# Extra matmuls on zeros in layer 1, with weights at four places behind the moving operand

## The chip, the core and the metric

The kernel runs on one core of one Trainium2 chip. The metric is the device time of one execution in microseconds (us). The engines are TensorE (PE: matmuls, and PEld: its weight loads), VectorE (DVE), ScalarE (ACT), GpSimd (POOL) and SyncE (SP, which issues the large DMA transfers).

## The reference

The kernel computes two layers of a bidirectional encoder on a sequence of 256 positions of width 1024, all in float32. In each layer

```python
h = rms_norm(x, g_mix)
b_a, c_a, x_a, u_p, q, k, v, ga, gp, gt = split(h @ w_in)
y_a = short_conv_mixer(b_a, c_a, x_a, conv_w, w_a_out)
y_p = multiscale_pool_mixer(u_p, w_pool, pool_scale)
y_t = windowed_gqa(q, k, v, rel_bias, sink) @ w_attn_out
x = x + (sigmoid(ga) * y_a + sigmoid(gp) * y_p + sigmoid(gt) * y_t) @ w_o
gate, up = split(rms_norm(x, g_ffn) @ w_gu)
x = x + (silu(gate) * up) @ w_down
```

and after both layers one more RMS norm. The input projection `w_in` is 1024 x 8704, and the feed-forward width is 2816.

## The kernel before, in words

Activations are held transposed: 128 features on the partitions, all 256 positions along the free dimension. A weight tile is a block of 128 x 128. One product of PE takes such a block as its stationary operand (the weights) and a tile of 128 x 256 as its moving operand, and adds 128 x 256 to an accumulator in PSUM.

To keep float32 accuracy with the faster float32r format, each operand is split in two: `hi`, the value rounded to float32r (by ACT, line 139), and `lo`, the remainder (by DVE, line 140). `mm3` (lines 164 to 168) makes three products of each block: hi weights by hi data (line 166), hi by lo (167) and lo by hi (168). The weights come from DRAM in the order of use, 16 blocks to a transfer (`dma_chunk`, issued by SP), and are split 8 blocks at a time (`convert`). Three buffers hold raw chunks, five each hold `hi` and `lo` parts. The order of the weights is a plan written out by `plan_layer`; `take` walks through it.

In the addresses of the built program every weight block of `mm3` stands 64 bytes past its moving operand, counted modulo 128 bytes; a padding of 112 columns ahead of `x` (line 89) takes part in that. The weights of the attention products (lines 356, 357 and 400) stand 0 bytes past it, modulo 128.

A layer begins in `mixer`. `quad_outer` makes the key and value projections of the not yet normed activations `xg`; `norm_stats` follows with two short products by a column of ones (`ps<-ones`, line 288; the trace records each twice) and a chain of small operations on DVE and ACT, whose result is the factor of the norm. Then come the eight query tiles (`CQ`). Behind the first of them in layer 1, behind the second in layer 0, `norm_rows` spreads the factor over the partitions with four more products (line 304). Then come the gates, the convolution, pooling and attention, interleaved, and the feed-forward part. The order of instructions on each engine is set by a scheduler that goes by the order of the code; `issue_after` ties a piece of code to the place behind a given instruction.

Temporary tiles of 128 x 512 floats share a pool named `t2` with eight buffers that are handed out in turn (line numbers here and below are those of before, unless they are said to be of after). The PSUM accumulators come from two pools, `psA` and `psB`, of four banks each.

Of the kernel before, what the change touches and what calls it, by code (L numbers as in the profile page):

```python
# [8 lines left out]
F32 = mybir.dt.float32  # L9
F32R = mybir.dt.float32r  # L10
# [6 lines left out]
P = 128  # L17
D = 1024
T = 256
# [73 lines left out]
def trunk(ctx, tc, wst, xT, sinkb, rb, invc, gfin, ident_d, out):  # L93
    nc = tc.nc
    V, S, G, PE = nc.vector, nc.scalar, nc.gpsimd, nc.tensor
# [5 lines left out]
    tmp = ctx.enter_context(tc.tile_pool(name="tmp", bufs=2))  # L101
# [5 lines left out]
    def nm(s):  # L107
        uid[0] += 1
        return f"{s}{uid[0]}"
# [60 lines left out]
    last_mm = [None]  # L170

    def half(j):
        return slice(j * T, (j + 1) * T)
# [68 lines left out]
    def pair(pool, tag, bufs, name):  # L242
        t = pool.tile([P, 2, T], F32R, name=nm(name), tag=tag, bufs=bufs)
        return t[:, 0, :], t[:, 1, :]
# [27 lines left out]
    def preload(func, src):  # L272

        d = tmp.tile([P, 1], F32, name=nm("pre"), tag="pre", bufs=2)
        S.activation(d, src, func)

    def rsqrt(r, sd, ms):

        V.reciprocal(r, sd)
        V.tensor_tensor(ms, ms, r, op=ALU.mult)  # L280
        V.tensor_tensor(ms, ms, r, op=ALU.mult)
        V.tensor_scalar(ms, ms, -0.5, 1.5, op0=ALU.mult, op1=ALU.add)
        V.tensor_tensor(r, r, ms, op=ALU.mult)

    def norm_stats(st, func):
        ps = psA.tile([P, 2 * T], F32, name=nm("ps"), tag="A")
        for tb in range(2):
            PE.matmul(ps[:, tb:tb + 1], st["sum"][:, tb * P:(tb + 1) * P], ones, start=True, stop=True)
        q = tmp.tile([P, 8], F32, name=nm("nq"), tag="nq", bufs=2)
        S.activation(q[:, 0:2], ps[:, 0:2], AF.Sqrt, bias=epst, scale=1.0 / D)  # L290
        V.tensor_scalar(q[:, 2:4], ps[:, 0:2], 1.0 / D, EPS, op0=ALU.mult, op1=ALU.add)
        preload(func, q[:, 0:1])
        rsqrt(q[:, 4:6], q[:, 0:2], q[:, 2:4])
        rr = tmp.tile([P, 4], F32R, name=nm("rr"), tag="nr", bufs=2)
        V.tensor_copy(rr[:, 0:2], q[:, 4:6])
        V.tensor_tensor(rr[:, 2:4], q[:, 4:6], rr[:, 0:2].bitcast(F32), op=ALU.subtract)
        st["q"], st["ps"] = rr, ps
# [94 lines left out]
    def att_pv(t, st):  # L392
        pts = st["pt"].pop(t)
        ps = newA("o")
        pr = t // 4
        for j in range(2):
            for kt in range(2):
                vv = vt[kt][:, pr, 2 * j:2 * j + 2].rearrange("p a d -> p (a d)")
                for i in range(2):
                    PE.matmul(ps[:, half(j)], vv, pts[kt][i][:, half(j)], start=(kt == i == 0), stop=(kt == i == 1))  # L400
        h, lo = pair(act, "q", 9, "ao")
        f, o = t1("of"), t1("oo")
        for j in range(2):
            r, other = slice(64 * j, 64 * j + 64), slice(64 - 64 * j, 128 - 64 * j)
            S.activation(o[r], ps[other, half(j)], AF.Copy)
            V.tensor_tensor(f[r], o[r], ps[r, half(j)], op=ALU.add)
        split(h, lo, f)
        st["ao"][t] = (h, lo)


    def t1(name):
        return tmp.tile([P, T], F32, name=nm(name), tag="t1", bufs=10)

    def mixer(l, st):
        xg = st["xg"]
        def kv_out():
            norm_rows(st)
            r = st["r"]

            for p in range(2):  # L420
                kf = t1("kf")
                V.tensor_tensor(kf[:, ::-1], kb[:, half(p)], r, op=ALU.mult)
                for j in range(2):
                    rr = slice(64 * j, 64 * j + 64)
                    other = slice(64 - 64 * j, 128 - 64 * j)
                    kh, kl = kk[2 * p + j]
                    split(kh[rr], kl[rr], kf[rr])
                    S.activation(kh[other], kf[rr], AF.Copy)
            vf = []
            for p in range(2):  # L430
                f = t1("vf")
                V.tensor_tensor(f[:, ::-1], vb[:, half(p)], r, op=ALU.mult)
                vf.append(f)
            return r, vf
# [2 lines left out]
        ast = {"s": {}, "pt": {}, "ao": {}, "bias": {t: load_bias(t) for t in range(3)}}  # L437
        if l:
            norm_stats(st, AF.Exp)
        qs = []  # L440
        for qd in range(2):
            banks = [newB(), newB()]
# [8 lines left out]
            for b in range(2):  # L451
                f = tmp.tile([P, 2, T], F32, name=nm("qf"), tag="t2", bufs=8)
                for j in range(2):
                    V.scalar_tensor_tensor(f[:, j], banks[b][:, half(j)], HEAD_SCALE, r, op0=ALU.mult, op1=ALU.mult)
                    qa, qb = pair(act, "q", 9, "q")
# [40 lines left out]
        for n in range(8):  # L496
# [5 lines left out]
            c, y, z = t1("c"), t1("y"), t1("z")  # L502
# [207 lines left out]
    with tc.issue_after(st["add"].ins):  # L710
        build_bias()
    for l in range(L):
        acc = mixer(l, st)
        st = {"xg": []}
        for j in range(4):
# [56 lines left out]
    assert state["pos"] == len(plan)  # L772


HEAD_SCALE = 0.125
WARM = 25
MH = 1
# [70 lines left out]
```

## Time and profile before

| | before |
|---|---|
| median of 2 runs | 966.3 us (965.72 to 966.88) |
| the profiled execution | 965.28 us |
| its span, first to last instruction | 963.1 us |
| PE busy | 952.8 us, 7881 products |
| DVE busy | 711.3 us |
| ACT busy | 551.0 us |
| DMA | 178.17 MB, 185 GB/s in the mean |

The span is shorter than the execution's time by what lies before the first and after the last instruction. A product on PE is recorded with some 0.28 us although the next starts after less than half of that: they overlap, so the step from one start to the next is what a product costs. Names in the profile leave out buffer numbers: `b<-xg,hi` is a product into a bank `b` of data `xg` and weights `hi`.

### The profile page before, as it was taken

Reading aid. Unit: us, or ns where it says so; the run is one execution under the profiler, and the core shown is the slowest. Engines: PE = TensorE matmul, PEld = TensorE weight load, DVE = VectorE, ACT = ScalarE, POOL = GpSimd, SP = SyncE. Lnnn points to the kernel's source line nnn. Section 1 sums busy time; section 2 is a strip of 40 time slices with the busy share of each in tenths; the row PEclk is TensorE's granted clock in tenths of the full one; section 3 lists DMA queues with packets and bytes.
Section 4 is the critical chain, followed back from the end, with each engine's and each line's share of the span. In section 5 each row is a group of like instructions: output and inputs, shape, how many; then the busy total and the mean of one; then the engine's idle time right before and its main releaser. Section 6 shows DMA issues by size and latency. Waiting matters only on the chain.

```text
span 963.1 us, 19117 instructions
## 1 busy us (share of the span) xinstructions
PE 952.8 (99%) x7881; PEld 939.9 (98%) x7881; DVE 711.3 (74%) x1277; ACT 551.0 (57%) x916; POOL 38.8 (4%) x60
## 2 busy tenths in 40 slices
PE   8999999999999999999999999999999999999997
PEld 8999999999999999999999999999999999999996
DVE  7999998577679955545599998975677698555555
ACT  6866777655456644444477666765545575444444
POOL 5000000000001000000020000000000020000000
PEclk9999999999999999999999999999999999999999
DMA  8656545544554555555543745444555455655541
GB/s 300 251 186 210 202 162 173 198 176 176 203 191 174 178 190 200 179 177 194 197 178 132 246 166 185 148 171 175 181 197 192 176 190 182 218 176 187 197 142 44
DMA packets 26967, 178.17 MB, mean 185 GB/s; under 512 B 3136, under 2 KB 3664, under 8 KB 6656
## 3 DMA queue, kind: packets, MB, share of 16 engines
q1 hardware_dynamic: 24768, 169.99, 49.8%
q0 software_dynamic: 2112, 6.97, 2.5%
q8 instruction: 61, 1.00, 0.4%
q14 instruction: 26, 0.21, 0.1%
HBM read 175.86 MB, written 1.08 MB: 184 GB/s over the span
## 4 chain that ended last, share of the span: by engine, by line
PE 98%; DMA 1%; DVE 0%; ACT 0%; SPq 0%; issue 0%
PE b L167 25%; PE b L166 25%; PE b L168 25%; PE dn L166 2%; PE dn L168 2%; PE dn L167 2%; PE dn L628 2%; PE dn L627 2%; PE dn L626 2%; PE wo L167 2%; PE wo L166 2%; PE o L400 2%; PE wo L168 2%; PE pt L385 1%; PE sc L357 1%; PE sc L356 1%
## 5 line engine op out<-in xcount | busy, mean ns | idle before, releaser
L140 DVE TENSOR_TENSOR lo<-raw,hi 128x1024 fp32r<-128x1024 f32 (+1 forms) x322 | 389.5, 1218 | 200.9 <-ACT hi L139 199.9
L139 ACT ACTIVATE hi<-raw 128x1024 fp32r<-128x1024 f32 (+1 forms) x322 | 335.9, 1051 | 308.4 <-PE b L167 189.7
L166 PE MATMUL b<-h,hi 128*128 128x256 f32 x1344 | 377.4, 281 | 0.0
L168 PE MATMUL b<-h,lo 128*128 128x256 f32 x1344 | 376.0, 280 | 0.0
L167 PE MATMUL b<-h,hi 128*128 128x256 f32 x1344 | 376.0, 280 | 0.0
L166 PEld LDWEIGHTS b<-h,hi 128*128 128x128 f32 x1344 | 255.0, 190 | 0.2
L168 PEld LDWEIGHTS b<-h,lo 128*128 128x128 f32 x1344 | 253.9, 189 | 0.0
L167 PEld LDWEIGHTS b<-h,hi 128*128 128x128 f32 x1344 | 252.4, 188 | 0.2
L166 PE MATMUL b<-xg,hi 128*128 128x256 f32 x448 | 125.2, 280 | 0.9 <-DVE xg L253 0.9
L167 PE MATMUL b<-xg,hi 128*128 128x256 f32 x448 | 124.9, 279 | 0.9 <-DVE xg L256 0.9
L168 PE MATMUL b<-xg,lo 128*128 128x256 f32 x448 | 124.7, 278 | 0.2 <-DVE lo L140 0.2
L167 PEld LDWEIGHTS b<-xg,hi 128*128 128x128 f32 x448 | 84.2, 188 | 1.3 <-DVE xg L256 1.3
L166 PEld LDWEIGHTS b<-xg,hi 128*128 128x128 f32 x448 | 84.2, 188 | 1.1 <-ACT hi L139 1.0
L168 PEld LDWEIGHTS b<-xg,lo 128*128 128x128 f32 x448 | 84.6, 189 | 0.4 <-DVE lo L140 0.4
L166 PE MATMUL dn<-fa,hi 128*128 128x256 f32 x176 | 49.5, 281 | 0.0
L167 PE MATMUL dn<-fa,hi 128*128 128x256 f32 x176 | 49.5, 281 | 0.0
L168 PE MATMUL dn<-fa,lo 128*128 128x256 f32 x176 | 49.5, 281 | 0.0
L369 ACT ACTIVATE s<-s,sm 128x256 f32<-128x256 f32 x64 | 31.7, 497 | 17.5 <-DVE sm L364 17.5
L166 PE MATMUL b<-z,hi 128*128 128x256 f32 x128 | 36.3, 284 | 0.0
L168 PE MATMUL b<-z,lo 128*128 128x256 f32 x128 | 36.0, 281 | 0.0
L166 PE MATMUL b<-ao,hi 128*128 128x256 f32 x128 | 36.0, 281 | 0.0
L167 PE MATMUL b<-ao,hi 128*128 128x256 f32 x128 | 36.0, 281 | 0.0
(176 smaller groups left out, 1494.1 us busy)
## 6 DMA issues: line engine op xcount, KB each, us to landing
raw<-wst SPq DMA_DIRECT2D x158, 1024.0 KB, 4.9
bias<-stab POOLq DMA_DIRECT2D x16, 384.0 KB, 4.5
raw<-wst SPq DMA_DIRECT2D x3, 512.0 KB, 8.0
out<-yg SPq DMA_DIRECT2D x4, 256.0 KB, 2.2
x<-xT SPq DMA_DIRECT2D x3, 256.0 KB, 8.0
raw<-wst SPq DMA_DIRECT2D x2, 256.0 KB, 5.1
gf<-gfin POOLq DMA_DIRECT2D x2, 256.0 KB, 3.1
x<-xT SPq DMA_DIRECT2D x1, 232.0 KB, 2.7
```

Source lines behind the costliest of these rows:

```text
L139: S.activation(hi[:, s], raw[:, s], AF.Copy)
L140: V.tensor_tensor(lo[:, s], raw[:, s], hi[:, s].bitcast(F32), op=ALU.subtract)
L166: PE.matmul(dst, wh, xh, start=start, stop=False, skip_group_check=skip)
L167: PE.matmul(dst, wh, xl, start=False, stop=False, skip_group_check=skip)
L168: last_mm[0] = PE.matmul(dst, wl, xh, start=False, stop=stop, skip_group_check=skip)
L356: PE.matmul(ps[:, half(j)], qs[t][j][:, cs], kh, start=True, stop=False)
L357: PE.matmul(ps[:, half(j)], qs[t][j][:, cs], kl, start=False, stop=True)
L369: S.activation(ss[i // 2][:, i % 2], ss[i // 2][:, i % 2], AF.Exp, bias=sm[:, 4 + i:5 + i], accum_out=sm[:, 12 + i:13 + i])
L400: PE.matmul(ps[:, half(j)], vv, pts[kt][i][:, half(j)], start=(kt == i == 0), stop=(kt == i == 1))
L626: PE.matmul(d, ah[:, cs], wh, start=(k == 0), stop=False)
L627: PE.matmul(d, ah[:, cs], wl, start=False, stop=False)
L628: PE.matmul(d, al[:, cs], wh, start=False, stop=(k == FT - 1))
```

## The change

A new function `probes` is called once, in layer 1, behind the key and value projections. It sets three tiles of zeros from the pool `t2` (za, zb, zc) with DVE, takes one bank of `psA`, and issues 598 products of zeros by zeros into it. They are 46 groups of 13. A group begins with one product whose moving operand has f columns, with f from 176 to 256 (line 420 of after); twelve products of 256 columns follow (line 423 of after). The weights are cut from zb or zc, w columns of 4 bytes past the tile's start, or a multiple of 128 columns further, and the moving operand from za at column 0 or 256. All three tiles stand alike modulo 128 bytes, so the weights stand 4 w bytes past the moving operand, modulo 128: 52, 60 and 68 bytes for w = 13, 15 and 17 (five groups each, f from the list SOME), 64 bytes for w = 16 (31 groups, f mostly from MANY). Every product starts and stops its own accumulation, and nothing reads the bank.

```diff
+    def probes():
+        za, zb, zc = [tmp.tile([P, 2 * T], F32R, name=nm("z"), tag="t2", bufs=8) for _ in range(3)]
+        for z in (za, zb, zc):
+            V.memset(z.bitcast(F32), 0.0)
+        a = newA("pa")
+        for w, firsts in PROBES:
+            for f in firsts:
+                PE.matmul(a[:, :f], zb[:, w:w + P], za[:, :f], start=True, stop=True)
+                for j in (0, 1, 2, 0):
+                    for t, m in ((zb, 0), (zb, T), (zc, 0)):
+                        PE.matmul(a[:, T:], t[:, w + j * P:w + (j + 1) * P], za[:, m:m + T], start=True, stop=True)
...
         if l:
             norm_stats(st, AF.Exp)
+        if l:
+            with tc.issue_after(last_mm[0].ins):
+                probes()
...
+SOME = (256, 248, 240, 224, 200)
+MANY = (252, 244, 236, 232, 228, 220, 216, 208, 192, 176)
+PROBES = ((13, SOME), (15, SOME), (17, SOME), (16, MANY), (16, (248,) + MANY), (16, MANY))
```

On PE, at the start of layer 1, the rows of before are the end of the key and value projections (into `b`), the short norm products (`ps<-ones`), and the first query tile:

```order
L166 MATMUL b_6213<-xg_6204,hi_6214 128x256
L167 MATMUL b_6213<-xg_6204,hi_6214 128x256
L168 MATMUL b_6213<-xg_6204,lo_6215 128x256
L288 MATMUL ps_6336<-ones,s_6210 128x1 x2
L166 MATMUL b_6352<-xg_6172,hi_6244 128x256
L167 MATMUL b_6352<-xg_6172,hi_6244 128x256
L168 MATMUL b_6352<-xg_6172,lo_6245 128x256
```

In after the rows at the same place are (`z` are the tiles of zeros, `pa` is the bank; `x2` stands for two equal rows):

```order
L166 MATMUL b_6213<-xg_6204,hi_6214 128x256
L167 MATMUL b_6213<-xg_6204,hi_6214 128x256
L168 MATMUL b_6213<-xg_6204,lo_6215 128x256
L288 MATMUL ps_6336<-ones,s_6210 128x1 x2
L420 MATMUL pa_6358<-z_6352,z_6353 128x256
L423 MATMUL pa_6358<-z_6352,z_6353 128x256 x2
L423 MATMUL pa_6358<-z_6352,z_6354 128x256
L423 MATMUL pa_6358<-z_6352,z_6353 128x256 x2
```

All 598 stand between the norm products and the first query tile.

On DVE, at the same time, the rows of before are the end of the layer's scaled activations (`xg`), weight splits (`lo`), and the beginning of the norm arithmetic (`nq`):

```order
L256 SCALAR_TENSOR_TENSOR xg_6204<-x,xg_6204 128x256
L140 TENSOR_TENSOR lo_6245<-raw_6141,hi_6244 128x1024
L140 TENSOR_TENSOR lo_6273<-raw_6141,hi_6272 128x1024
L140 TENSOR_TENSOR lo_6303<-raw_6242,hi_6302 128x1024
L140 TENSOR_TENSOR lo_6355<-raw_6242,hi_6354 128x1024
L140 TENSOR_TENSOR lo_6411<-raw_6300,hi_6410 128x1024
L291 TENSOR_SCALAR nq_6339<-ps_6336 128x2
```

In after three memsets stand among them:

```order
L256 SCALAR_TENSOR_TENSOR xg_6204<-x,xg_6204 128x256
L416 MEMSET z_6352 128x512
L140 TENSOR_TENSOR lo_6245<-raw_6141,hi_6244 128x1024
L140 TENSOR_TENSOR lo_6273<-raw_6141,hi_6272 128x1024
L140 TENSOR_TENSOR lo_6303<-raw_6242,hi_6302 128x1024
L416 MEMSET z_6353 128x512
L416 MEMSET z_6354 128x512
L140 TENSOR_TENSOR lo_6960<-raw_6242,hi_6959 128x1024
```

The first memset stands ahead of three splits, the other two behind them; the rest of DVE's order is the same, with other buffer numbers.

## The prediction

> **What bounds the kernel now.** I read the page from the top: the busy times, the granted clock, and the chain of work that ended last.
>
> ```profile
> span 963.1 us, 19117 instructions
> PE 952.8 (99%) x7881; PEld 939.9 (98%) x7881; DVE 711.3 (74%) x1277; ACT 551.0 (57%) x916; POOL 38.8 (4%) x60
> ...
> PEclk9999999999999999999999999999999999999999
> ...
> PE 98%; DMA 1%; DVE 0%; ACT 0%; SPq 0%; issue 0%
> ```
>
> TensorE (PE) is 98% of the chain, and its clock is full throughout. Next, the view of waits for PE alone, to see how much of its time is spent on anything but its own products.
>
> ```profile
> PE wps L184 <- DVE epst L179: 1.2, 1, 1.2
> PE b L167 <- DVE xg L256: 0.9, 2, 0.6
> PE b L166 <- DVE xg L253: 0.9, 1, 0.9
> PE b L168 <- DVE lo L140: 0.2, 1, 0.2
> ```
>
> That is 3.2 us of waiting in the whole run; all idle time of PE is 963.1 - 952.8 = 10.3 us. PE issues product after product, in order, so a product added in the middle pushes everything behind it back by its own step. What matters is that step, not the duration that the profile gives a product (0.28 us), since products overlap. I read the step from a view of stretches that hold nothing but 256-column products: length over count. Each product is 0.28 us long, so about 2.4 more are counted in a stretch than start in it.
>
> ```profile
> core 0: us, PE busy (x), PEclk, DMA share, GB/s
> 172.00:290.00 118.00, 118.00 (x1004) 1.00 0.53 187
> 502.00:530.00 28.00, 28.00 (x250) 1.00 0.42 148
> 311.00:490.00 179.00, 179.00 (x1521) 1.00 0.52 182
> 646.00:765.00 119.00, 119.00 (x1013) 1.00 0.53 186
> ```
>
> 28.00 / 247.6 is 113.1 ns; 179.00 / 1518.6 is 117.9 ns; 118.00 / 1001.6 and 119.00 / 1010.6 are both 117.8 ns. So the same kind of product runs at one of two steps, and keeps it for hundreds of products. The clock is 1.00 in all four, and DMA traffic is lowest in the quick stretch but not by much. In the built program the weights of all these products stand 64 bytes past the moving operand, counted modulo 128. Other forms of product, from the timeline of PE:
>
> ```profile
> 578.90 0.28 PE L400 MATMUL o<-ph,vt 128*128 128x256 f32 x1
> ...
> 579.74 0.28 PE L400 MATMUL o<-pl,vt 128*128 128x256 f32 x1
> 585.51 1.03 PE L385 MATMUL pt<-ident,s 128*128 128x128 f32 x8
> ...
> 944.80 0.39 PE L626 MATMUL dn<-hi,fa 128*128 128x512 f32 x1
> ...
> 952.81 0.39 PE L628 MATMUL dn<-hi,fa 128*128 128x512 f32 x1
> ```
>
> The first two rows are the first and last of eight products whose weights stand 0 bytes past the moving operand (modulo 128): 0.84 us over seven steps, 120 ns. The third holds eight products of 128 columns: at 0.27 us each, seven steps take 1.03 - 0.27 = 0.76 us, 109 ns. [...] The last two are the ends of 36 products of 512 columns: 8.01 us over 35 steps, 229 ns.
>
> **The change part by part.** It adds 46 groups of 13 products to PE: a first product (line 420) and twelve of 256 columns (line 423). Of the firsts, 3 have 256 columns and 43 have 176 to 252. Nothing is removed. The place is the start of layer 1, behind the key and value products and the short norm products (L288). This is the chain in order of time there; columns are start, length, what:
>
> ```profile
> 494.74 0.12 PE b L168
> 494.86 0.34 PE ps L288 x4
> 495.19 0.23 PE b L166
> 495.42 0.12 PE b L167
> ...
> 498.48 0.12 PE b L166
> 498.60 0.47 PE ps L304 x4
> ```
>
> PE is busy on both sides of 495.19 us, so nothing there can hide the added work; each step of it counts in full.
>
> *The 372 products at 64 bytes* (31 groups of w = 16, twelve each). They stand as the kernel's own products do, so they get one of that pair's steps: 113.1 or 117.9 ns. Which one I can't read off: the state seems to be set by what runs just ahead (in layer 1 the quick stretch starts right behind the norm products of 498.60 us), and the firsts differ in length so that some may set one and some the other. I take the middle, 115.5 ns: 372 x 115.5 = 43.0 us, with 42.1 and 43.9 as ends.
>
> *The 180 products at 52, 60 and 68 bytes* (15 groups). The only weights in the trace at such odd places are the broadcast columns of the four norm products of 498.60 us: 0.47 us, 117.5 ns each. The other near rows are 113.1 ns quick, 117.9 slow, and 120 at offset 0. I take 118.5, between the slow rows, as I see no reason for the best state there: 21.3 us, with 20.4 and 21.6 as ends.
>
> *The 46 firsts.* The 3 full ones at 117.9 are 0.4 us. The 43 short ones lie between the row of 128 columns (109 ns) and the quick step (113.1); I take 110: 4.7 us. Ends 4.7 and, at the slow step, 5.1.
>
> The sum is 43.0 + 21.3 + 0.4 + 4.7 = 69.4 us; the ends are 42.1 + 20.4 + 0.3 + 4.7 = 67.5 and 43.9 + 21.6 + 0.4 + 5.1 = 71.0.
>
> [...]
>
> *The three zero tiles* (line 416) are written by VectorE (DVE), and the first added product waits for them. DVE has the first memset ahead of three weight splits and the others behind them (its order stands in the section on the change). The times of the splits are in the timeline of DVE; the cost of a memset is in the list of groups:
>
> ```profile
> 488.45 2.40 DVE L256 SCALAR_TENSOR_TENSOR xg<-x,xg 128x256 fp32r<-128x256 f32 x2
> 490.77 4.62 DVE L140 TENSOR_TENSOR lo<-raw,hi 128x1024 fp32r<-128x1024 f32 x4
> 495.92 1.23 DVE L140 TENSOR_TENSOR lo<-raw,hi 128x1024 fp32r<-128x1024 f32 x1 [0.53 <-ACT hi L139]
> ...
> L212 DVE MEMSET kk<- 128x256 f32 x4 | 1.1, 272 | 0.0
> L179 DVE MEMSET epst<- 128x1 f32 x1 | 0.1, 59 | 0.0
> ```
>
> 256 columns take 272 ns and one takes 59, so 512 take about 0.49 us. The last memset ends at about 490.77 + 3 x 1.16 + 3 x 0.49 = 495.7 us; PE is there at 495.19. So it waits some 0.5 us: between 0 (the splits run a little earlier) and 0.9. The split and norm arithmetic queued on DVE behind the memsets serves products that now come 69 us later, so that delay reaches nobody. SP's weight loads and ScalarE's (ACT) roundings run into full buffers and stop; when PE goes on, they restart at the pace of before.
>
> *What follows.* The products behind the norm rows of 498.60 us run at 113.1 ns until 530 us. If the altered start throws those 280 into the slow step it costs 280 x 4.8 = 1.3 us. Further on both layers show 117.8 ns at the same place, though their transfers fall differently, so I expect no change there: 0, with -1 and +1.3 as ends.
>
> Sum: 69.4 + 0.5 = 69.9 us. The profiled execution took 965.28 us, 2.2 more than its span and 1.0 under the median of 966.3; from it the sum gives 1035.2, from the median **1036.2 us**, which I predict, 7.2% slower.
>
> **The rivals.** *Short products are dearer.* For it: the norm products are recorded twice as often as the program has them.
>
> ```profile
> L288 PE MATMUL ps<-ones,s 128*128 128x1 f32 x16 | 2.0, 229 | 0.0
> L184 PE MATMUL wps<-warm 128*128 128x256 f32 x25 | 4.8, 371 | 1.2 <-DVE epst L179 1.2
> ```
>
> The program holds 8 of these plain float32 products, the trace 16: PE does break some forms into passes. If float32r under 256 columns is broken in two, 43 x 110 ns add 4.7 us: 1040.9; in four, 14.2 us: 1050.4. Against it: the 128-column transposes run at 109 ns. But they are another operation. 10%.
>
> *Weights at odd places stall.* If a load at 52, 60 or 68 bytes takes as long as a 512-column product (229 ns), 180 x (229 - 118.5) adds 19.9 us: 1056.1. Against it stand only the 117.5 ns of the four norm products and the mildness of 113 against 120 ns for 64 against 0 bytes. 6%.
>
> *The products never run, and it is not slower.* Nobody reads their result, so a stage behind the built program could drop them; then the time stays at 966.3 us. It would decide from 73% dropped: 2% of 966.3 is 19.3 us, of 69.9. Against it: the 25 warm-up products (L184) are read by nobody either, and the trace has all 25. 2%.
>
> *The wait on the zero tiles grows.* If a buffer that a memset takes were still held, PE would stand; but the DVE rows show that it is through its splits by 495.4 us. Beyond 5 us, so over 1041: 2%.
>
> **How the numbers follow.** The forecast gets 80%. Its ends are 966.3 + 67.5 - 1 = 1032.8 and 966.3 + 71.0 + 0.9 + 1.3 = 1039.5. I widen them to 1032.5 and to 1042, so that short products in two passes (1040.9, about half of that rival) are inside: some 85%, with room for a size that I have off. This kernel's measurement can tell about 2% from no change. All cases but the dropped products are over that bound of 985.6: slower 0.98, same 0.02, faster 0.
>
> **What would show it.** In the after profile line 423 should have 552 products and line 420 46, with steps of 113 to 120 ns in the stretch from 495.7 to about 565 us; an idle of PE of 0.5 us at line 420, released by the memset of line 416; and the stretch behind it as it was at 495 us, shifted. Steps of 220 ns or more behind line 420 alone would mean broken short products; steps over 125 ns in the first 195 products alone would mean costly weights at odd places. A sum outside 67 to 72 us with each step inside 113 to 120 would make the downstream part wrong.

## The result, and the profile after

The changed kernel takes 1032.0 us (median of two runs, 1029.06 and 1034.97) against 966.3: a ratio of 1.068, with 1.055 to 1.081 as its interval. It is slower by over 2%, as forecast, but the time lies 0.5 us under the low end of the range. The profiled execution is the one of 1029.06 us; the step by step forecast for it was 1035.2. So some 6 us that the prediction counted are not there. (Below, quick stands for the step of 113 ns that the prediction read from the trace, slow for that of 118.)

The page of the changed kernel:

```profile
span 1027.3 us, 20320 instructions
PE 1016.3 (99%) x8479; PEld 1002.7 (98%) x8479; DVE 712.5 (69%) x1280; ACT 551.0 (54%) x916; POOL 38.4 (4%) x60
...
PEclk9999999999999999999999999999999999999999
...
PE 93%; DVE 3%; DMA 1%; ACT 1%; issue 1%; SPq 0%; DVEq 0%
...
L423 PE MATMUL pa<-z,z 128*128 128x256 f32 x552 | 69.9, 281 | 0.0
```

All 598 products ran (8479 - 7881), the granted clock is 0.998 and PE is still the chain (93%). But the span grew by 64.2 us only. The first place to look is the added stretch itself. The view of one line, for the first products of the groups, gives its ends, and the view of stretches its step:

```profile
L420 PE MATMUL pa<-z,z x46: 241/268/357, 489.3 to 557.7; 128*128 128x248 f32 x4, 128*128 128x256 f32 x3, 128*128 128x240 f32 x3, 128*128 128x224 f32 x3
```

```profile
core 0: us, PE busy (x), PEclk, DMA share, GB/s
314.00:484.00 170.00, 170.00 (x1502) 1.00 0.52 186
493.30:557.00 63.70, 63.70 (x548) 1.00 0.03 12
572.00:594.00 22.00, 22.00 (x196) 1.00 0.40 145
711.00:830.00 119.00, 119.00 (x1013) 1.00 0.51 185
```

The second stretch is the change: 63.70 / (548 - 2.4) is 116.8 ns a step. Start to start, the 598 products take 69.93 us, where the sum had 69.4. The two stretches behind it run at 113.6 and 117.8 ns, quick and slow as in before at those places. The first stretch is the surprise. It lies in layer 0's feed-forward part, 5 us before the first added product at its end and 175 at its start; 170.00 / (1502 - 2.4) is 113.4 ns. The same stretch in before:

```profile
core 0: us, PE busy (x), PEclk, DMA share, GB/s
314.00:484.00 170.00, 170.00 (x1446) 1.00 0.53 186
```

That is 117.8 ns. The first 4177 products of PE are the same in both kernels, in order and by their tiles, and yet 1560 of them, from the norm rows of that feed-forward part (310.9 us) to the place of the change, took 6.9 us less in this execution. Laid product against product, the two executions differ by +0.1 us up to those norm rows, -6.9 between them and the change, +70.9 at the change, +0.2 in the query tiles behind it and -0.2 at the start of layer 1's feed-forward part: 64.1 of the 64.2 us. The last two are no work of the change: before, profiled once more below, shows them too (+0.3 and -0.2) against the profile shown first.

At the head of the added stretch the views of waits, of the chain (in order of time) and of DVE's timeline show the step on the zero tiles:

```profile
PE pa L420 <- DVE z L416: 0.9, 1, 0.9
```

```profile
487.96 0.13 PE b L168
488.09 0.04 DVEq L140
488.13 0.48 DVE lo L140
488.61 0.05 issue
488.67 0.50 DVE z L416
489.16 0.14 issue
489.30 0.36 PE pa L420
```

```profile
484.78 0.48 DVE L416 MEMSET z<- 128x512 f32 x1
485.19 3.42 DVE L140 TENSOR_TENSOR lo<-raw,hi 128x1024 fp32r<-128x1024 f32 x3
488.67 1.03 DVE L416 MEMSET z<- 128x512 f32 x2
489.62 2.28 DVE L140 TENSOR_TENSOR lo<-raw,hi 128x1024 fp32r<-128x1024 f32 x2
```

PE starts its last own product at 488.17 us, where before did at 494.95, and DVE is 5.6 us early too. PE stands until the second memset is through. From its last own product to the first added one it takes 1.13 us, where before takes 0.11 to its next product: 1.02 more, 0.88 of it idle. The chain passes from PE to DVE here.

### The profile page after: what moved, and what is told of

Its sections match the earlier page's. It is cut to its first block, busy times and chain, and to the rows that moved or that the text cites. A ratio compares the mean times of both kernels' runs of the same rounds, so it can differ in the third digit from the quotient of the medians.

```text
span 1027.3 us, 20320 instructions
## 1 busy us (share of the span) xinstructions
PE 1016.3 (99%) x8479; PEld 1002.7 (98%) x8479; DVE 712.5 (69%) x1280; ACT 551.0 (54%) x916; POOL 38.4 (4%) x60
## 4 chain that ended last, share of the span: by engine, by line
PE 93%; DVE 3%; DMA 1%; ACT 1%; issue 1%; SPq 0%; DVEq 0%
PE b L167 22%; PE b L168 22%; PE b L166 22%; PE pa L423 6%; PE dn L646 2%; PE dn L645 2%; PE dn L168 2%; PE dn L644 2%; PE dn L167 2%; PE dn L166 2%; PE wo L166 1%; PE wo L167 1%; PE o L400 1%; PE wo L168 1%; DMA raw<-wst 1%; PE pt L385 1%
## 5 line engine op out<-in xcount | busy, mean ns | idle before, releaser
L423 PE MATMUL pa<-z,z 128*128 128x256 f32 x552 | 69.9, 281 | 0.0
L423 PEld LDWEIGHTS pa<-z,z 128*128 128x128 f32 x552 | 67.7, 189 | 0.1
```

Of the source, the lines that this page charges most:

```text
L423: PE.matmul(a[:, T:], t[:, w + j * P:w + (j + 1) * P], za[:, m:m + T], start=True, stop=True)
```

## The experiments

The question was why identical products ran 6.9 us quicker ahead of the change, and whether that belongs to the change. Two theories: (A) any execution of either kernel settles by itself into the quick or the slow step at layer 0's norm rows (those of its feed-forward part), and before and after were caught in different ones; (B) the change brings it about, through something that differs between the programs ahead of it (loads of code, buffers, transfers). The runs were taken in four sets, each on one chip and with before beside it: e1 to e4; e5, e6, e8, e9; e10 to e12; and e7, e13, e14. All kernels that insert products add zeros into a running sum, so the result is that of the reference's computation; the `probes` bank is read by nobody in any of them.

### Both kernels again

No edit, many executions of each.

> The kernel before, unchanged. Theory (state by chance): the some 1560 products between the norm rows of layer 0's feed-forward part and the place of the change run at 113.3 or 117.9 ns, chosen anew in each execution by where PE's short wait at the norm rows happens to end; so the times of one and the same program fall into two groups, near 966 and near 959 us. Rival (the change does it): nothing but the changed kernel gets the quick step there, and all times here are 965 to 967 us.

> The changed kernel, unchanged. Theory: two groups, near 1029 and near 1036 us, as in its two times so far (1029.06 and 1034.97). Rival (noise of the clock or of transfers): times spread evenly between 1029 and 1035, with the added stretch itself longer or shorter.

Before, 12 times: nine at 957.6 to 961.4 us, three at 965.6 to 966.8. After, 6 times: five at 1030.5 to 1031.0, one at 1036.6. With the runs of before beside all sets it has 70 executions: 57 lie at 957.5 to 961.7 (mean 959.6), thirteen at 965.6 to 968.3 (mean 966.7), none between, and each group has granted clocks of 0.997 to 0.999. The two shown before the prediction were both of the rarer, upper group. The groups are 7.2 us apart; 1560 products by 4.6 ns are 7.2. Of before an upper execution was profiled again; after's was a lower one:

```profile
314.00:484.00 170.00, 170.00 (x1446) 1.00 0.53 186
```

```profile
314.00:484.00 170.00, 170.00 (x1502) 1.00 0.53 187
```

The first row is of before again (966.81 us), the second of after again (1030.65). So both kernels have both times with nothing altered, and (B) isn't needed. Another stretch differs between the two profiles of before: some 300 products behind the norm rows of layer 1's feed-forward part, quick in the first and slow in the second, 1.3 us. No unchanged execution of before in its lower group was profiled; the nearest are kernels with a few products added, below, and each of those at 959 to 961 us has 1502 or 1503 products in this stretch. Lower group against lower group, in this set, the change costs 1030.7 - 959.6 = 71.1 us; the upper groups, of which after has only two executions, give 1035.8 - 966.7 = 69.1.

### One product to set the step

If a short product can move PE between the steps, one put into each feed-forward part, just behind the norm rows, might remove the two groups. The products use the warm-up tile of zeros as weights.

```diff
 in mm3, ahead of the first product:
+        if not start and not stop and key in KICKS:
+            PE.matmul(dst[:, :KICK], warm[:, 24:24 + P], xh[:, :KICK], start=False, stop=False, skip_group_check=skip)
...
+KICK = 252
+KICKS = ((0, "gu", 4, 3), (1, "gu", 4, 3))
```

> The kernel before with one added product of 252 columns, zero weights 64 bytes past the moving operand, in each layer's feed-forward part, a dozen products behind the norm rows; it adds zeros to a running sum. Theory: this first of 252 columns puts PE in the quick state every time, as it did in the added groups; 1556 products x 4.6 ns = 7.2 us less, all times 958 to 960 us. Rival: 966.5 us, or still two groups.

> The changed kernel with the same two added products. Theory: one group, near 1029 us, and against the pinned kernel before a difference of 70 to 71 us, which is the price of the change. Rival: two groups again, or a difference well under 70.

On before: 958.1 to 960.1 us five times, 966.4 to 967.5 seven times, still two groups. On after: four times 1036.4 to 1037.7, and a 1032.5 that fits neither group and has no profile. The profiles show why. In the one of before (959.42 us) PE came from the norm rows with steps of 117 and 118 ns and left the added product with 113; in the one of after (1037.47) it came with 113 and 114 and left with 117 and 118. The product doesn't set a step, it changes it: slow to quick, quick to slow. So a single product of 252 columns can decide the next 1500 steps.

### Pairs, and the same in after

In after's own added stretch some groups of twelve were quick (113.3 ns), those behind firsts of 252, 232, 220 and 192 columns at 64 bytes and of 248, 224 and 200 at 52 bytes. From there came the next device: 236 columns, and seven products later 252, behind the norm rows of both mixers and both feed-forward parts and behind the last attention step of each layer.

```diff
 in mm3, ahead of the first product:
+        if key in KICKS:
+            due[:] = [236, 0, 252]
+        if due and not start and not stop:
+            f = due.pop(0)
+            if f:
+                PE.matmul(dst[:, :f], warm[:, 24:24 + P], xh[:, :f], start=False, stop=False, skip_group_check=skip)
 in the attention steps:
+                    if f is att_pv and t == 7:
+                        due[:] = [236, 0, 252]
...
+KICKS = ((0, "gu", 4, 3), (1, "gu", 4, 3), (0, "in", 4, CQ + 2), (1, "in", 4, CQ + 1))
```

> The kernel before with six pairs of added products that add zeros to a running sum: one of 236 columns, and seven products later one of 252. A pair stands behind the norm rows of each mixer and of each feed-forward part, and behind the last attention step of each layer. Theory (a short first shifts the phase: 236 always leaves the slow step, 252 turns slow into quick): after each pair PE is at 113.3 ns. Layer 0's feed-forward stretch is then quick in every execution, and the some 940 products behind the last attention step, at 118 ns in all profiles so far, gain 2 x 940 x 4.7 ns = 8.8 us; 12 added products cost 1.4 us; so one group of times, 950 to 953 us. Rival (the state can't be set from the program): two groups, 960 and 967 us.

> The changed kernel with the same six pairs. Theory: one group of times, and 70 to 71 us over the kernel before with the pairs, that is 1021 to 1024 us: the price of the change with the chance taken out. Rival: two groups, or a difference under 67.5 us, the low end of my sum.

Before: 967.1 to 969.5 us, four of four; beside it plain before was at 957.5 to 960.0 seven times of seven. After: 1037.7 to 1039.3, four of four. The groups are gone, but on the slow side: in the profiles PE is quick behind each 236 at the norm rows, and each 252 throws it out; behind the attention it stayed slow through both (117.8 ns in both layers), so the 8.8 us expected there were not gained. Layer 0's feed-forward stretch in after with the pairs:

```profile
314.00:484.00 170.00, 170.00 (x1446) 1.00 0.52 188
```

This speaks for (A): here the added products of layer 1 stand as they do in after, and the stretch ahead of them is slow in the profile, and by the times in all four executions, through a product placed ahead of it. With the state set alike the change costs 1039.2 - 968.6 = 70.6 us.

### The firsts: all 252, all 236

```diff
-PROBES = ((13, SOME), (15, SOME), (17, SOME), (16, MANY), (16, (248,) + MANY), (16, MANY))
+PROBES = ((16, (252,) * 46),)
```

and the same with 236. These leave out the other three places of the weights.

> The changed kernel with all 46 groups at 64 bytes and begun by 252 columns. Theory (a shift of phase): such a first turns slow into quick and quick into slow, so groups alternate, and the added stretch takes 46 x 0.116 + 552 x 0.1155 = 69.1 us. Rival (the length of the first sets the state, whatever it was): all groups at 113.3 ns, 67.9 us.

> The changed kernel with all 46 groups at 64 bytes and begun by 236 columns. Theory (236 ends in quick and stays there): after at most four groups all are at 113.3 ns, and the added stretch takes 46 x 0.105 + 46 x 0.122 + 506 x 0.1133 = 67.8 us. Rival (with the zero tiles' addresses some slow phase is kept): groups at 118 ns throughout, 70.2 us.

Up to the first added product the two kernels and after have the same products in the same order. The layer 0 stretch came quick in the one of 252 (the first row, 1030.87 us) and slow in the one of 236 (1036.47):

```profile
314.00:484.00 170.00, 170.00 (x1503) 1.00 0.53 190
314.00:484.00 170.00, 170.00 (x1446) 1.00 0.53 189
```

With e8 below, which came quick (x1502), this is the strongest evidence for (A): the change stands in all three, and the stretch ahead of it takes either step.

The added stretch took 69.6 us with 252 and 68.0 with 236. In PE's timeline, three groups in a row with firsts of 252, and one with 236:

```profile
520.35 0.28 PE L420 MATMUL pa<-z,z 128*128 128x252 f32 x1
520.47 1.58 PE L423 MATMUL pa<-z,z 128*128 128x256 f32 x12
521.88 0.28 PE L420 MATMUL pa<-z,z 128*128 128x252 f32 x1
522.00 1.52 PE L423 MATMUL pa<-z,z 128*128 128x256 f32 x12
523.36 0.27 PE L420 MATMUL pa<-z,z 128*128 128x252 f32 x1
523.47 1.57 PE L423 MATMUL pa<-z,z 128*128 128x256 f32 x12
```

```profile
519.96 0.27 PE L420 MATMUL pa<-z,z 128*128 128x236 f32 x1
520.06 1.53 PE L423 MATMUL pa<-z,z 128*128 128x256 f32 x12
```

Twelve products last eleven steps and 0.28 us: (1.52 - 0.28) / 11 is 113 ns, 1.58 gives 118. With 252 one group in three is quick, in a cycle, not every second one as expected; so the slow step isn't one state but more than one, which look alike until the next short product. With 236 every group is quick from the second on: the short product takes 105 ns, the next one 122, and then the step is 113 again.

### The place of the weights

```diff
+PROBES = tuple((w, (252, 244, 236, 232, 228, 256)) for w in (0, 4, 8, 14, 16, 18, 20, 24))
```

> The changed kernel with the weights at 0, 16, 32, 56, 64, 72, 80 and 96 bytes behind the moving operand, six groups at each, begun by 252, 244, 236, 232, 228 and 256 columns: 48 groups, 624 products. Theory (two steps at each place, and the best step depends on the place): 64 bytes shows 113.3 and 117.9 ns; 0 bytes no better than 120, as the attention products; odd eighths between. Rival (only the firsts matter, not the place): 113.3 and 117.9 ns at all eight places.

These are 624 products, with the weights at eight places; the stretch took 73.7 us. By place, the steps of the last six products of a group were 118 to 120 ns at 0 bytes, 118 to 119 at 16 and at 32, 116 to 119 at 56, 117.5 to 119 at 72, 118.5 to 119 at 80, 117 to 119 at 96. At 64 bytes they were 113.3 behind two of the six firsts (252 and 232), and about 118 behind the others. In the timeline, the first of these rows is a group at 0 bytes, the next two are at 64, the last at 96:

```profile
497.97 1.60 PE L423 MATMUL pa<-z,z 128*128 128x256 f32 x12
...
528.62 1.52 PE L423 MATMUL pa<-z,z 128*128 128x256 f32 x12
530.09 1.58 PE L423 MATMUL pa<-z,z 128*128 128x256 f32 x12
...
553.04 1.60 PE L423 MATMUL pa<-z,z 128*128 128x256 f32 x12
```

So in these groups the quick step hangs on the place of the weights as well as on the short product ahead. Of the places tried it was reached at 64 bytes, and in after's groups at 52; six firsts at a place can't prove that the others never reach it.

### One 236, and a scan of lengths

If 236 columns leave or make PE quick, one of them behind each of the four norm rows should leave only the lower group (the edit of the pairs, with `due[:] = [236]`, and nothing behind the attention). The third kernel adds to this, on before and behind the last attention step, single products of fourteen lengths in layer 0 and of six lengths three times each in layer 1, 31 to 64 products apart.

> The kernel before with one added product of 236 columns, zeros onto a running sum, some dozen products behind the norm rows of each mixer and each feed-forward part (four in all). In the profiles of the pairs, the product of 236 at these places was followed by the quick step each time, whatever came before, and it was the 252 behind it that undid this. Theory: layer 0's feed-forward stretch is quick in every execution, one group of times at 957 to 961 us, none at 965 or above. Rival: two groups, as before.

> The changed kernel with the same four products of 236 columns. Theory: one group at 1029 to 1031 us, and 70 to 71 us over the kernel before with the same four. Rival: two groups near 1030 and 1037 us.

> The kernel before with the four products of 236, and in the long slow stretch behind each layer's last attention step (some 930 products) short products of zeros onto running sums, 30 to 50 products apart: in layer 0 one each of 252, 248, 244, 240, 236, 232, 228, 224, 220, 216, 208, 200, 192 and 176 columns, in layer 1 three each of 232, 224, 240, 252, 216 and 248. Theory (a short product shifts the phase, and the step that follows hangs on where the phase was): some of them are followed by 113.3 ns until the next one, among them at least one of the three of 252. Rival (these products, whose operands differ from the zero tiles', can't reach the quick step here): 117.5 to 119 ns throughout.

Before with one 236: 958.2 to 961.3 us eight times, 965.2 to 966.4 four times. After: 1028.4 to 1030.7 three times, 1036.2 to 1038.6 three times. Two groups again, and the expectation fell: in the profile of before one of the four places went slow to slow across its 236. The scan (one execution, 961.28 us) has its first added product here, on PE's timeline, between steps of 118 ns and steps of 113.5:

```profile
184.64 0.28 PE L172 MATMUL b<-h,hi 128*128 128x256 f32 x1
184.76 0.28 PE L173 MATMUL b<-h,hi 128*128 128x256 f32 x1
184.88 0.28 PE L174 MATMUL b<-h,lo 128*128 128x256 f32 x1
185.00 0.28 PE L171 MATMUL b<-h,warm 128*128 128x252 f32 x1
...
186.93 0.28 PE L173 MATMUL b<-h,hi 128*128 128x256 f32 x1
```

From 185.00 to 186.93 there are 17 products, 113.5 ns each, where the same place in before is slow. From the quick step, products of 236, 224 and 220 columns left PE quick; 252, 248, 240, 232, 216 and 176 threw it out. From the slow step the same length sometimes brought the quick one and sometimes didn't: of layer 1's threes the second 232, the third 224, the second 240, the first 252 and the second 216 did, and three 248 in a row did not. So 236 keeps the quick step wherever it was seen, and one of several 236 in a row might bring it.

### Four 236

```diff
+        if key in KICKS:
+            due[:] = [236, 0, 0] * 4
...
+                    if f is att_pv and t == 7:
+                        due[:] = [236, 0, 0] * 4
```

Four products of 236 columns, 10 to 20 products from one to the next, at the six places of the pairs, 24 in all.

> The kernel before with four products of 236 columns, some nine products apart, behind the norm rows of each mixer and feed-forward part and at the last attention step of each layer (24 added in all). In the profiles so far a product of 236 left the quick step quick (7 of 7) and took the slow step to quick in some cases and not in others. Theory (slow has several phases, each 236 moves on to the next, and quick is where they end): four in a row end in the quick step wherever they begin; layer 0's feed-forward stretch is quick every time, and the two stretches behind the last attention steps gain 2 x 4.3 us against 24 x 0.11 us: one group of times, 952 to 955 us. Rival (some slow phase is kept by 236): two groups again, or the stretches behind attention stay at 118 ns and all times are 961 us and over.

> The changed kernel with the same 24 products. Theory: one group of times, and 70 to 71 us over the kernel before with the same 24: 1023 to 1026 us. That difference is the price of the change, with the state of the stretch ahead of it set alike. Rival: two groups, or a difference outside 67.5 to 73 us.

Before: 952.4 to 954.7 us, six of six, while plain before beside it had eight at 958.5 to 960.9 and three at 966.5 to 967.5. After: 1023.8 to 1024.4, five of five. One group each, and both on the quick side. In before with the four:

```profile
core 0: us, PE busy (x), PEclk, DMA share, GB/s
186.00:290.00 104.00, 104.00 (x919) 1.00 0.54 189
314.00:484.00 170.00, 170.00 (x1503) 1.00 0.53 187
652.00:752.00 100.00, 100.00 (x885) 1.00 0.54 192
```

The first and the last row, 113.5 and 113.3 ns, are the places behind the attention that were at 117.8 in the prediction's rows. At five of the six places the third 236 at the latest brought the quick step, and the next kept it; behind layer 0's first norm rows four other products stand ahead of the last 236, and PE leaves it slow. It is the best kernel of the study: 953.7 us in the median, 0.992 (0.989 to 0.995) of plain before beside it with both its groups. That is under the 2% that this comparison can call, but the six lie below all eleven of before. The account against the lower group: 917 products behind the attention in each layer, 1834 by 4.4 ns, are 8.1 us, less 24 x 0.11 = 2.6 for the added products: 5.5 as an estimate, where 959.9 - 953.7, with the lower group of this set, is 6.2.

The price of the change with the state set alike, in one group each, is 1024.1 - 953.7 = **70.4 us**.

## Why the prediction was right or wrong

*The products at 64 bytes: right.* 43.7 us for 372, against 43.0 and within its ends; 117.4 ns each where the middle of the two steps, 115.5, was taken. Only four lengths of first reached 113 (252, 232, 220 and 192), and the product right behind a short one takes longer.

*The products at 52, 60 and 68 bytes: right in sum, partly by luck.* 21.4 us for 180, against 21.3; 118.0, 120.5 and 118.8 ns by place. But the figure at 52 bytes includes the start of the stretch, where steps of 138 and 224 ns stand (135 to 142 and 222 to 224 in e6, e7 and e8, which start at 64 or 0 bytes). Without the first group the products at 52 bytes take 115.5 ns, and some are quick, which the prediction saw no reason to expect; the slower ones at 60 bytes and that start made up for it. The rival of stalls (229 ns) is out. Against the 117.4 ns at 64 bytes, 60 and 68 are 2.6 and 1.2% over, and 52 without its first group is 1.6% under.

*The firsts: right in sum, not as pictured.* The 43 short ones took 4.4 us, 102 ns each, and the 3 full ones 0.4. But the product behind a short one takes 128 ns: a first of 176 columns took 78, its successor 150. What a short product saves, the next one gives back, and the pair stays at 230 ns. So the 109 ns of the 128-column products is no lower bound for a single step. Broken passes (the 10% rival) are out. The sum of the three terms is 69.9 us (after again: 69.9 too), where 69.4 was forecast.

*The wait on the zero tiles: right, with two sizes.* PE is idle for 0.88 us in the profiled execution, where 0.5 was forecast with 0.9 as its end. The size goes with layer 0's step: 0.9 in all six profiles of changed kernels where that was quick, and 0.2 in the three where it was slow, as the forecast assumed. The rivals of a longer wait and of products that never run are out.

*Behind the change: right, by and large.* Some 64 query products behind the norm rows were slow (118 ns) where the prediction's rows of before are quick (113.1), then the quick step came back: +0.2 us. In before profiled again the same products are slow as well. The weight transfers moved 145 and 185 GB/s in the two stretches behind the change, where the prediction's rows of before have 148 and 186.

*What failed is the base, the step from the sum to the time.* The prediction laid 69.9 us on 966.3 as if the rest of the kernel were one number, and gave its ends (-1 and +1.3) only to what lies behind the change. The rows that it quoted said otherwise: the same products at 113.1 or 117.9 ns, a step kept for hundreds of products, set by what runs just ahead. It drew from them a range for the added products, but not for the kernel's own, and took two runs 1.2 us apart for the whole of the spread. In its place the runs show two bases, 959.6 and 966.7 us, with layer 0's 1560 products as the 7.2 us between them. Laid on the lower one, 69.9 us more give 1029.5, and on the upper one 1036.6; the two runs of after are 1029.06 and 1034.97. It was bad luck that both runs of the base fell into the group that has 13 of 70 executions, and that after's two fell into different ones: two runs in the upper group, at some 1035.8, would have been inside the range. The median of 1032.0 is the middle between two groups, a time that hardly any execution has. The prediction's own last check did point there (a growth outside 67 to 72 us with each step between 113 and 120 ns), but "downstream" was the wrong side: the difference lay ahead of the change.

*What stays open.* What decides, in a given execution, which step PE has behind layer 0's norm rows. The first norm product (`ps<-ident,rr`) takes its weights from a small tile that DVE writes just ahead; in all sixteen profiles its weight load starts 51 to 54 ns behind the end of that write. In ten of them the product is held: it starts 138 to 153 ns behind the one ahead of it, and the second norm product 220 to 223 ns later. Behind 140 (twice), 141 (twice) and 153 ns PE came out quick, behind 138, 145, 149, 150 and 152 slow. In the other six nothing is held (118 or 119 ns, then 117 or 118), and all six came out quick. In PE's timeline the first two rows are of before, held and then slow, the last two of after again, not held and then quick; two products last one step and 0.28 us, so the second starts 0.22 us behind the first in before and 0.12 in after again:

```profile
310.72 0.28 PE L166 MATMUL b<-xg,hi 128*128 128x256 f32 x1
310.86 0.50 PE L304 MATMUL ps<-ident,rr 128*128 128x256 f32 x2
...
312.60 0.28 PE L166 MATMUL b<-xg,hi 128*128 128x256 f32 x1
312.71 0.40 PE L304 MATMUL ps<-ident,rr 128*128 128x256 f32 x2
```

So the hold and its length seem to decide, but sixteen executions are too few for a rule, and what makes the hold come and go isn't shown. That the two steps are a phase, as the expectations have it, was the author's guess: the cycle of three fits it, but no trace shows such a phase.

## What to carry to other kernels

Before a cost is laid on a base, run the base often enough to see whether it has one time or two: a median of two can lie in the rarer group, and one of mixed groups is a time of neither. Where the profile shows the same product at two steps, every stretch of it is a term with two values, those ahead of the change too; compare two traces product by product, from the start, before explaining a difference by the change. And where long runs of equal matmuls stand in the slower step, a few short products between them may be worth trying: 24 of them, by estimate 2.6 us of added work, brought this kernel to 953.7 us, 6.2 under the lower of its two groups, and left one group.

## What the runs showed of the hardware

- Float32r products of 128 x 128 by 128 x 256 back to back, with the weights 64 bytes behind the moving operand modulo 128, take 113.3 or 117.8 ns a step, at a granted clock of 0.997 to 0.999. Either is kept for over 1500 products, and either can stand in the same place of the same program in two executions (the some 300 products behind the norm rows of layer 1's feed-forward part, in the two profiles of before).
- One product with fewer columns can move PE from one step to the other, and it saves little: with its successor it takes 230 ns in the mean (43 pairs in after). 236 columns kept the quick step each time; 252 took it from quick to slow each time, and in a row of groups begun by 252 alone one in three was quick.
- The two plain float32 products of one column at the start of layer 1 (`ps<-ones`, each recorded twice) take 0.34 us of before's chain, 170 ns each, where a float32r product of 256 columns takes 113 or 118.
- The place of the weights behind the moving operand, modulo 128 bytes, matters: 113 ns was seen at 64 and at 52 bytes; 116 to 121, as means of a group's last six, at 0, 16, 32, 56, 60, 68, 72, 80 and 96.
- Behind the norm rows of layer 0's feed-forward part the quick step followed in all six profiles where the norm products were not held, and in five of the ten where they were.
